# Attention values with the value tile stationary, two heads per bank, divided by reciprocal rows that travel through a DRAM scratch tensor

## The chip, the cores and the metric

The kernel runs on 1 core of one Trainium2 chip. The metric is device time in microseconds (us), the median of several runs. The span of a profiled execution is the stretch from its first to its last recorded instruction. Engines are named as in the profile: PE (TensorE matmul), PEld (TensorE weight load), DVE (VectorE), ACT (ScalarE), POOL (GpSimd), SP (SyncE, which issues the loads).

## The reference, cut to what matters

A trunk of two layers over 256 tokens of width 1024. Each layer is a feed-forward block (width 2816), a token mixer and a second feed-forward block; the mixer of the first layer is latent attention, that of the second a state-space scan. The change lies in the attention, 16 heads, 96 features for queries and keys and 64 for values:

```python
def one_block(args):          # two blocks of 128 queries
    q_blk, i = args
    s = einsum('bhqd,bhkd->bhqk', q_blk, kt) * scale
    s = where(k_pos[None, :] <= q_pos[:, None], s, -inf)
    p = softmax(s, axis=-1)
    return einsum('bhqk,bhkd->bhqd', p, vt)
...
return o.reshape(Bn, S, H * Dv) @ w_o
```

The mixer's result is the 256 x 1024 attention output times a 1024 x 1024 matrix `w_o`.

## The kernel before, in words

Activations are kept as features by tokens (128 features on the partitions, 256 tokens along the row). Large products split both operands into a high and a low half and take three matmuls (`mm3`: high by high, high by low, low by high). Weights come in 1 MiB loads on SP's queue, are cast by ACT (L206) and their low half is formed by DVE (L207). The conditioning vectors of later blocks are worked out beside all this in pieces of one DVE instruction each (`ada_half`, L237).

Order of the work: each engine runs a fixed list of instructions in order. That list is laid out when the kernel is built, by a planner that goes by its own estimate of when each instruction's inputs are ready; the order of the code is the priority, not the order itself. The helper lines L295 and L300 hold every matmul and every transpose, L206 and L207 every split into halves.

The attention runs in turns `turn(t)`, one head begun per turn. Head h gets its scores in turn h (`scores`: queries by keys, into one PSUM bank), its softmax in turn h+1 (`softmax`: row maxima on DVE, exponentials on ACT, whose accumulators give the denominators `DEN`, queries on the partitions), its three transposes of 128 x 128 probabilities in turn h+2 (`probs_t`), the copy of these out of PSUM in turn h+3 (`probs_evac`), and its products with the values in turn h+4 (`values`).

`values(h)` holds the transposed probabilities stationary (128 x 128) and moves 64 columns of the values: three products, whose result is queries by features. Four heads (a "quad") share one bank. `o_evac(quad)` (turn 4 quad + 8) takes the reciprocal of the denominators (L1058) and multiplies the whole bank by it (L1060), `o_t(quad)` turns the result into features by queries with four transposes, and `o_split(quad)` splits it into halves (L206, L207) that enter the product with `w_o`.

Turns 0 to 18 are written ahead of `down`, turns 19 to 22 are hooks inside it. `down(s, 8, ...)` makes the eight 128-row chunks m of `w_o`'s product; each has eight steps k, and step k takes `OT[k]`, two heads' output. Chunks 0 and 1 first do steps k = 0 to 5, with the hooks after every second step, and after all hooks their steps 6 and 7, which need the last quad. Chunks 2 to 7 follow whole. After each chunk `leave_chunk` (L460) and `enter_chunk` (L409 to L411, L399) update the residual and prepare the next block on DVE, ACT and POOL.

PSUM has eight banks, one tag for all uses. The scan of the second layer has a product `ymm`, L1309 to L1317, that the change resembles: it holds 64 columns of a value-like tile stationary and writes one head of a pair to partitions 0 to 63 of a bank and the other to 64 to 127.

Of the kernel before, what the change touches and what calls it, by code (L numbers as in the profile page):

```python
# [7 lines left out]
F32 = mybir.dt.float32  # L8
F32R = mybir.dt.float32r
# [3 lines left out]
ALU = mybir.AluOpType  # L13
# [3 lines left out]
T = 256  # L17
# [5 lines left out]
HEADS = 16  # L23
# [31 lines left out]
class Piece:  # L55


    def __init__(self, hi, lo):
        self.hi, self.lo = hi, lo
# [5 lines left out]
class Trunk:  # L65
    def __init__(self, ctx, tc, a, out):
        self.tc, self.nc, self.a, self.out = tc, tc.nc, a, out
        self.p = ctx.enter_context(tc.tile_pool(name="sb", bufs=1))
        self.ps_pool = ctx.enter_context(
            tc.tile_pool(name="ps", bufs=8, space=bass.MemoryType.PSUM))  # L70
        self.uid = 0
        self.pin = False

# [635 lines left out]

    def mla_setup(self):  # L710
        nc = self.nc
        self.qag = self.cst["latg"]
        rowg = self.cst["qkg_row"].rearrange("p (a d) -> p a d", a=2)
        inv = self.cst["inv"]
# [8 lines left out]
                                in1=inv.rearrange("p (o d) -> p o d", o=1).broadcast_to([128, 2, 16]), op=ALU.mult)  # L723
# [92 lines left out]
    def mla(self, s):  # L816
        nc = self.nc
# [27 lines left out]
        q = [self.latent(qp[0], R, 2)]  # L845
# [5 lines left out]
        for c in range(2):  # L851
            self.transpose(out=krp[:, c * 32:(c + 1) * 32], in_=kr[0:32, c * 128:(c + 1) * 128],
                                identity=self.ident[0:32, 0:32])
# [62 lines left out]
        KT, QT, V = [], {}, [[None, None], [None, None]]  # L916

        def kt_evac(banks):
            for b in banks:
                KT.append(self.heads_evac(b, self.gcol[0:96, 0:1]))  # L920
# [75 lines left out]
        QT[0] = [self.heads_evac(b, None) for b in qb]  # L996
        q_evac(1, 1, p1)

        SC, PB, PTs, O, DEN, OT, ON, OB = {}, {}, {}, {}, {}, [], {}, {}

        def scores(h):
            quad, hh = divmod(h, 4)
# [10 lines left out]
        def softmax(h):  # L1013
            quad, hh = divmod(h, 4)
            if hh == 0:
                DEN[quad] = self.small([128, 2, 4], "den", 3)
            cq = CQ[quad]
            ps = SC[h]
            mx = self.small([128, 2], "mx", 4)
            nc.vector.reduce_max(out=mx[:, 1:2], in_=ps[:, 0:256], axis=AX.X)  # L1020
            nc.vector.reduce_max(out=mx[:, 0:1], in_=ps[:, 256:384], axis=AX.X)
            nc.vector.scalar_tensor_tensor(out=mx, in0=mx, scalar=-1.0, in1=cq[:, :, hh], op0=ALU.mult, op1=ALU.mult)
            P = self.t3()
            for c, sl in ((1, slice(0, 256)), (0, slice(256, 384))):
                nc.scalar.activation(out=P[:, sl], in_=ps[:, sl], func=AF.Exp, bias=mx[:, c:c + 1],  # L1025
                                     scale=cq[:, c, hh:hh + 1], accum_out=DEN[quad][:, c, hh:hh + 1])
            SC[h] = P

        def probs_t(h):
            P = SC.pop(h)  # L1030
            pp = PB[h] = self.bank()
            for b in range(3):
                self.transpose(out=pp[:, b * 128:(b + 1) * 128], in_=P[:, b * 128:(b + 1) * 128],
                                    identity=self.ident)

        def probs_evac(h):
            PTs[h] = self.t3()
# [2 lines left out]
            else:  # L1040
                nc.vector.tensor_copy(out=PTs[h], in_=PB.pop(h)[:, 0:384])  # L1041

        def values(h):
            quad, hh = divmod(h, 4)
            half, h8 = divmod(h, 8)
            if hh == 0:
                O[quad] = self.bank()
            PT = PTs.pop(h)
            hc = slice(h8 * 64, (h8 + 1) * 64)
            o0 = O[quad][:, hh * 64:(hh + 1) * 64]  # L1050
            o1 = O[quad][:, 256 + hh * 64:256 + (hh + 1) * 64]
            self.matmul(o1, PT[:, 0:128], V[0][half][:, hc], start=True, stop=False)
            self.matmul(o1, PT[:, 128:256], V[1][half][:, hc], start=False, stop=True)
            self.matmul(o0, PT[:, 256:384], V[0][half][:, hc], start=True, stop=True)

        def o_evac(quad):
            den = DEN.pop(quad)
            nc.vector.reciprocal(out=den, in_=den)  # L1058
            t = ON[quad] = self.slot()
            nc.vector.tensor_tensor(  # L1060
                out=t.rearrange("p (c h d) -> p c h d", c=2, d=64),
                in0=O.pop(quad).rearrange("p (c h d) -> p c h d", c=2, d=64),
                in1=den.rearrange("p c (h o) -> p c h o", o=1).broadcast_to([128, 2, 4, 64]), op=ALU.mult)

        def o_t(quad):
            t = ON.pop(quad)
            ps = OB[quad] = self.bank()
            for b in range(2):
                for c in range(2):
                    self.transpose(out=ps[:, b * 256 + c * 128:b * 256 + (c + 1) * 128],  # L1070
                                        in_=t[:, c * 256 + b * 128:c * 256 + (b + 1) * 128], identity=self.ident)

        def o_split(quad):
            ps = OB.pop(quad)
            hi, lo = self.slot(F32R), self.slot(F32R)
            self.split_pair(hi, lo, ps)
            for b in range(2):
                OT.append((hi[:, b * T:(b + 1) * T], lo[:, b * T:(b + 1) * T]))

        def turn(t):  # L1080

            quad, hh = divmod(t, 4)
            nq = quad + 2
            if t < HEADS and hh == 0:
                if quad == 0:
                    kt_evac(b3)
                    q_rstd(1)
                if nq < 4:
                    turn.p0 = q_proj(nq, 0)
            if 0 <= t - 3 < HEADS:  # L1090
                probs_evac(t - 3)
            if 0 <= t - 1 < HEADS:
                softmax(t - 1)
            if t >= 8 and t % 4 == 0:
                o_evac(t // 4 - 2)
            if t >= 10 and t % 4 == 2:
                o_split(t // 4 - 2)
            if t < HEADS:
                scores(t)
            if nq < 4:  # L1100
                if hh == 1:
                    q_evac(nq, 0, turn.p0)
                    turn.p1 = q_proj(nq, 1)
                if hh == 2:
                    q_evac(nq, 1, turn.p1)
                if hh == 3:
                    q_rstd(nq)
            if 0 <= t - 2 < HEADS:
                probs_t(t - 2)
            if 0 <= t - 4 < HEADS:  # L1110
                values(t - 4)
            if t >= 9 and t % 4 == 1:
                o_t(t // 4 - 2)
            if quad + 1 < 4:
                if hh == 1:
                    turn.qb = quad_t(QQ[quad + 1])
                if hh == 2:
                    QT[quad + 1] = [self.heads_evac(b, None) for b in turn.qb]

        tail = HEADS + 3  # L1120
        for t in range(tail):
            turn(t)

        def last(t):
            turn(t)
            self.ada_half(2)
        rest = [lambda t=t: last(t) for t in range(tail, HEADS + 7)]
        self.down(s, 8, lambda k: OT[k], rest, 2, 2, 1, MLA_EVERY)


# [513 lines left out]
```

## Time and profile before

| | |
|---|---|
| median of 3 runs | 1076.95 us (1076.59 to 1077.67) |
| profiled execution, its own time | 1077.47 us |
| its span | 1075.7 us |
| PE busy | 1059.3 us, 98% of the span |
| DVE busy | 871.9 us, 81% |
| ACT busy | 617.5 us, 57% |
| POOL busy | 40.0 us, 4% |
| attention turns, by the trace | about 250 to 290 us into the span |

Busy time of PE is modelled: matmuls overlap, so the distance from one group's start to the next group's start is the better measure of what a group costs. In a row of a timeline the number in front is the start, then the length, and "x6" says how many instructions were merged; the bracket tells how long the engine had been idle before it and what ended that. All DMAs of this kernel are issued by SP and run on one queue.

### The profile page before, as it was taken

What the parts mean: (1) busy time and instruction counts of PE and PEld (TensorE: products, weight loads), DVE (VectorE), ACT (ScalarE), POOL (GpSimd) and SP (SyncE); (2) the same over time, 40 slices, a digit from 0 to 9 for tenths busy, and PEclk for the clock granted to TensorE, in tenths of its full rate; (3) what the DMA queues carried; (4) which work ended last, traced back from release to release, by engine and by line L of the source; (5) the groups of instructions that cost most, each with busy time, mean ns of one, the idle gap of its engine ahead of it and who ended that gap; (6) DMA issues with size and microseconds to landing.
All of it is one profiled execution on the core that took longest, in us unless ns stands there. A gap on an engine that the chain in (4) does not pass through costs nothing.

```text
span 1075.7 us, 21725 instructions
## 1 busy us (share of the span) xinstructions
PE 1059.3 (98%) x8814; PEld 1042.9 (97%) x8814; DVE 871.9 (81%) x1551; ACT 617.5 (57%) x1099; POOL 40.0 (4%) x102
## 2 busy tenths in 40 slices
PE   6999999999999999999999999999999999999998
PEld 5999999999999999999999999999999899999998
DVE  5899988889989878766999886599999788756642
ACT  5564544479567454444745444498889566544431
POOL 0000000000010000100000000000210000000000
PEclk9999999999999999999999999999999999999999
DMA  9999898754266887875699887554344454666630
GB/s 349 334 368 347 338 374 310 286 199 150 100 232 225 325 306 292 290 271 199 240 362 350 334 321 257 171 180 157 119 137 157 157 183 171 240 221 217 231 131 21
DMA packets 38264, 259.59 MB, mean 241 GB/s; under 512 B 4370, under 2 KB 5522, under 8 KB 8084
## 3 DMA queue, kind: packets, MB, share of 16 engines
q1 hardware_dynamic: 38164, 258.21, 65.9%
q8 instruction: 69, 1.13, 0.4%
q14 instruction: 31, 0.25, 0.1%
HBM read 257.14 MB, written 1.05 MB: 240 GB/s over the span
## 4 chain that ended last, share of the span: by engine, by line
PE 93%; DMA 3%; DVE 2%; ACT 1%; issue 0%; SPq 0%; ACTq 0%
PE bank L295 92%; DMA raw<-in_adao_dram 3%; PE bank L300 1%; DVE raw L259 1%; DMA raw<-in_xt_dram 0%; ACT sl L813 0%; ACT t L1025 0%; DVE wlo L618 0%; ACT whi L206 0%; DVE ssq L947 0%; ACT t L942 0%; DVE wlo L207 0%; DVE mx L1020 0%; ACT sl L811 0%; DVE t L1041 0%
## 5 line engine op out<-in xcount | busy, mean ns | idle before, releaser
L295 PE MATMUL bank<-sl,whi 128*128 128x256 f32 (+2 forms) x5360 | 954.7, 282 | 5.2 <-ACT sl L652 4.0
L295 PEld LDWEIGHTS bank<-sl,whi 128*128 128x128 f32 (+1 forms) x5360 | 818.0, 188 | 8.6 <-ACT sl L652 5.0
L295 PE MATMUL bank<-sl,wlo 128*128 128x256 f32 (+2 forms) x2680 | 746.3, 280 | 0.0
L206 ACT CAST whi<-raw 128x1024 fp32r<-128x1024 f32 (+1 forms) x329 | 340.8, 1041 | 304.2 <-PE bank L295 217.3
L295 PEld LDWEIGHTS bank<-sl,wlo 128*128 128x128 f32 (+1 forms) x2680 | 503.5, 188 | 0.2
L207 DVE TENSOR_TENSOR wlo<-raw,whi 128x1024 fp32r<-128x1024 f32 (+1 forms) x329 | 398.0, 1214 | 90.4 <-ACT whi L206 88.3
L237 DVE SCALAR_TENSOR_TENSOR raw<-raw,cb 128x1024 f32<-128x1024 f32 x128 | 154.7, 1220 | 25.4 <-DMA raw<-in_adaw_dram 25.2
L329 ACT CAST sl<-t 128x256 fp32r<-128x256 f32 x125 | 48.7, 405 | 32.6 <-DVE t L526 24.4
L330 DVE TENSOR_TENSOR sl<-t,sl 128x256 fp32r<-128x256 f32 x125 | 51.2, 419 | 1.0 <-ACT sl L329 0.7
L460 DVE SCALAR_TENSOR_TENSOR x<-bank,mod,x 128x256 f32<-128x256 f32 x48 | 22.9, 480 | 21.8 <-PE bank L295 21.6
L410 ACT ACTIVATE sl<-x,scol 128x256 fp32r<-128x256 f32 x40 | 20.3, 508 | 33.4 <-DVE x L460 33.3
L526 DVE TENSOR_TENSOR t<-t,bank 128x256 f32<-128x256 f32 x70 | 28.8, 417 | 12.5 <-PE bank L295 12.5
L1164 DVE SCALAR_TENSOR_TENSOR sl<-t,cst,sl 128x256 f32<-128x256 f32 x72 | 35.1, 495 | 0.1
L525 ACT ACTIVATE t<-bank 128x256 f32<-128x256 f32 x70 | 26.0, 380 | 0.0
L295 PE MATMUL bank<-whi,sl 128*128 128x384 f32 (+1 forms) x80 | 24.3, 368 | 0.0
L259 DVE SCALAR_TENSOR_TENSOR raw<-raw,cb 128x1024 f32<-128x1024 f32 x16 | 19.6, 1222 | 5.6 <-DMA raw<-in_adao_dram 5.5
L409 POOL CAST sl<-bspl 128x4 fp32r<-128x4 f32 x40 | 11.8, 343 | 318.7 <-PE bank L295 232.1
L1302 ACT ACTIVATE dec<-sl,nac 128x128 f32<-128x128 f32 x64 | 20.6, 399 | 4.9 <-DVE sl L1291 4.8
L411 DVE SCALAR_TENSOR_TENSOR sl<-x,scol,sl 128x256 fp32r<-128x256 f32 x40 | 19.3, 482 | 4.2 <-ACT sl L410 4.1
L440 POOL TENSOR_TENSOR rr<-rv,mhalf 128x2 f32<-128x2 f32 x11 | 11.2, 1019 | 304.2 <-DVE rv L436 304.2
L423 ACT ACTIVATE t<-t,mod,scol 128x256 f32<-128x256 f32 x32 | 18.4, 596 | 4.0 <-DVE t L422 4.0
L618 DVE TENSOR_TENSOR wlo<-raw,whi 128x1024 fp32r<-128x1024 f32 (+1 forms) x17 | 19.5, 1156 | 0.0
(215 smaller groups left out, 652.8 us busy)
## 6 DMA issues: line engine op xcount, KB each, us to landing
raw<-in_wgu_dram SPq DMA_DIRECT2D x80, 1024.0 KB, 5.6
raw<-in_adaw_dram SPq DMA_DIRECT2D x64, 1024.0 KB, 5.9
raw<-in_wdn_dram SPq DMA_DIRECT2D x44, 1024.0 KB, 6.0
raw<-in_win_dram SPq DMA_DIRECT2D x19, 1024.0 KB, 5.0
raw<-in_wout_dram SPq DMA_DIRECT2D x8, 1024.0 KB, 4.9
raw<-in_wop_dram SPq DMA_DIRECT2D x6, 1024.0 KB, 6.7
raw<-in_adao_dram SPq DMA_DIRECT2D x6, 1024.0 KB, 8.4
raw<-in_mwo_dram SPq DMA_DIRECT2D x4, 1024.0 KB, 4.9
```

Source lines behind the costliest of these rows:

```text
L206: self.nc.scalar.copy(out=hi, in_=raw)
L207: self.nc.vector.tensor_tensor(out=lo, in0=raw, in1=hi.bitcast(F32), op=ALU.subtract)
L237: nc.vector.scalar_tensor_tensor(out=w, in0=w, scalar=1.0, in1=self.cb, op0=ALU.mult, op1=ALU.mult, accum_out=self.mod[:, q, 2 * u + i:2 * ...
L259: self.order(nc.vector.scalar_tensor_tensor(out=w, in0=w, scalar=1.0, in1=self.cb, op0=ALU.mult, op1=ALU.mult, accum_out=self.mod[:, q, c]))
L295: ins = self.nc.tensor.matmul(*a, **k)
L329: self.nc.scalar.copy(out=hi, in_=src)
L330: self.nc.vector.tensor_tensor(out=lo, in0=src, in1=hi.bitcast(F32), op=ALU.subtract)
L460: nc.vector.scalar_tensor_tensor(out=self.x[m], in0=ps[:, 0:T], scalar=self.mod[:, q, m:m + 1], in1=self.x[m], op0=ALU.mult, op1=ALU.add)
L525: nc.scalar.activation(out=tg, in_=pg[:, 0:T], func=AF.Silu)
L526: nc.vector.tensor_tensor(out=tg, in0=tg, in1=pu[:, 0:T], op=ALU.mult)
L1164: nc.vector.scalar_tensor_tensor(out=dst, in0=u[:, t:t + T], scalar=cw[:, t:t + 1], in1=dst, op0=ALU.mult, op1=ALU.add)
L1302: self.order(nc.scalar.activation(out=t[:, j, 2 * c], in_=q[:, o:o + 128], func=AF.Exp, bias=self.nac[:, c, h:h + 1]))
```

## The change

The products are turned round. `values(pair)` takes two heads: the values (128 keys x 64 features) are stationary and the transposed probabilities move, 256 columns for the first 128 keys and 128 columns for the second. The two heads of the pair write partitions 0 to 63 and 64 to 127 of one bank, so the result is features by queries and needs no transpose: `o_t`, `o_split` and their four transposes per quad are gone. `probs_t` writes its three blocks in another order, so that the moving columns are contiguous. A pair is taken in every odd turn from turn 5.

The division must now vary along the row instead of along the partition. `divisors(quad)` (turn 4 quad + 5) takes the reciprocals and sends them from POOL's queue, in two DMAs, to a scratch tensor `dend` in DRAM laid out as head by query: 128 partitions x 4 single values each, 512 pieces of 4 bytes per DMA. Two more DMAs read it back, each row broadcast to 64 partitions (64 partitions x 2 rows of 256 values). `o_evac(quad)` (turn 4 quad + 8, as before) then multiplies two banks by these rows and splits the product. The hooks are turns 17 to 20 instead of 19 to 22.

```diff
-            self.matmul(o1, PT[:, 0:128], V[0][half][:, hc], start=True, stop=False)
-            self.matmul(o1, PT[:, 128:256], V[1][half][:, hc], start=False, stop=True)
-            self.matmul(o0, PT[:, 256:384], V[0][half][:, hc], start=True, stop=True)
...
+        def values(pair):
+
+            ps = O[pair] = self.bank()
+            hs = [2 * pair, 2 * pair + 1]
+            PT = [PTs.pop(h) for h in hs]
+            for c in range(2):
+                for j, h in enumerate(hs):
+                    half, h8 = divmod(h, 8)
+                    self.matmul(ps[j * 64:(j + 1) * 64, c * 128:T], V[c][half][:, h8 * 64:(h8 + 1) * 64],
+                                PT[j][:, c * 256:256 + c * 128], start=(c == 0), stop=(c == 1))
+        def divisors(quad):
+
             den = DEN.pop(quad)
             nc.vector.reciprocal(out=den, in_=den)
...
+            d = self.dend[quad]
+            for c in range(2):
+                nc.gpsimd.dma_start(out=d.rearrange("h c q -> c q h")[c], in_=den[:, c])
+            t = DB[quad] = self.slot()
+            for j in range(2):
+                nc.gpsimd.dma_start(out=t[j * 64:(j + 1) * 64].rearrange("p (i l) -> p i l", i=2),
+                                    in_=d.rearrange("(i j) c q -> j i (c q)", j=2)[j].partition_broadcast(64))
+
+        def o_evac(quad):
+            t = self.slot()
+            for i in range(2):
+                ps = O.pop(2 * quad + i)
+                nc.vector.tensor_tensor(out=t[:, i * T:(i + 1) * T], in0=ps[:, 0:T], in1=DB[quad][:, i * T:(i + 1) * T],
+                                        op=ALU.mult)
+                if quad == 3:
+                    OT.append(self.split_act(t[:, i * T:(i + 1) * T]))
+            if quad < 3:
+                hi, lo = self.slot(F32R), self.slot(F32R)
+                self.split_pair(hi, lo, t)
...
-        tail = HEADS + 3
+        tail = HEADS + 1
...
-        rest = [lambda t=t: last(t) for t in range(tail, HEADS + 7)]
+        rest = [lambda t=t: last(t) for t in range(tail, HEADS + 5)]
```

## Rows read from the trace of the kernel before

**Rows 1.** The page: busy shares, forty slices, the chain that ended last.

```profile
PE 1059.3 (98%) x8814; PEld 1042.9 (97%) x8814; DVE 871.9 (81%) x1551; ACT 617.5 (57%) x1099; POOL 40.0 (4%) x102
PEclk9999999999999999999999999999999999999999
PE 93%; DMA 3%; DVE 2%; ACT 1%; issue 0%; SPq 0%; ACTq 0%
```

**Rows 2.** Busy time by stretch: length, PE, PEld, DVE, ACT, POOL, clock, DMA.

```profile
260.00:265.00 5.00, 4.98 (x39) 4.88 (x40) 4.28 (x15) 4.44 (x16) 0.00 (x0) 1.00 0.01 3
270.00:275.00 5.00, 4.95 (x42) 4.77 (x42) 4.82 (x20) 3.48 (x13) 0.00 (x0) 1.00 0.01 2
285.00:290.00 5.00, 4.72 (x43) 4.72 (x44) 4.62 (x10) 2.63 (x10) 0.67 (x7) 1.00 0.01 3
290.00:295.00 5.00, 5.00 (x45) 5.00 (x44) 4.88 (x10) 0.84 (x2) 0.00 (x0) 1.00 0.82 249
```

**Rows 3.** Chain that ended last, in order of time, attention's first turns.

```profile
257.86 0.47 DVE t L1041
...
267.93 0.42 DVE mx L1020
```

**Rows 4.** PE's timeline: value products of two turns, four transposes of `o_t`.

```profile
275.00 0.78 PE L295 MATMUL bank<-sl,t 128*128 128x64 f32 x6
276.76 0.78 PE L295 MATMUL bank<-sl,t 128*128 128x64 f32 x6
277.38 0.87 PE L295 MATMUL bank<-sl,sl 96*128 96x256 f32 x4
280.81 0.61 PE L300 MATMUL bank<-ident,sl 128*128 128x128 f32 x4
281.26 0.82 PE L295 MATMUL bank<-sl,sl 96*128 96x256 f32 x4
281.91 0.27 PE L295 MATMUL bank<-maskq,identb 128*128 128x256 bf16 x1
```

**Rows 5.** PE's timeline in the scan: one pair of `ymm` and its neighbours.

```profile
759.92 0.28 PE L295 MATMUL bank<-sl,wlo 128*128 128x256 f32 x1
760.12 0.87 PE L295 MATMUL bank<-dec,sl 128*64 128x256 f32 x8
760.93 0.50 PE L295 MATMUL bank<-sl,whi 128*128 128x256 f32 x2
761.26 0.29 PE L295 MATMUL bank<-sl,wlo 128*128 128x256 f32 x1
```

**Rows 6.** Groups by line and shape, 254 to 294 us: count, busy us, mean ns.

```profile
L295 PE MATMUL bank<-sl,t 128*128 128x64 f32 x96 | 13.0, 264 | 0.2 <-DVE t L1041 0.2
L237 DVE SCALAR_TENSOR_TENSOR raw<-raw,cb 128x1024 f32<-128x1024 f32 x6 | 7.2, 1219 | 0.0
L1060 DVE TENSOR_TENSOR sl<-bank,den 128x512 f32<-128x512 f32 x4 | 2.7, 687 | 0.2 <-PE bank L295 0.2
L300 PE MATMUL bank<-ident,sl 128*128 128x128 f32 x16 | 2.5, 273 | 0.0
```

**Rows 7.** The page's groups: 128x256 casts, halves and products from PSUM; POOL's power.

```profile
L329 ACT CAST sl<-t 128x256 fp32r<-128x256 f32 x125 | 48.7, 405 | 32.6 <-DVE t L526 24.4
L330 DVE TENSOR_TENSOR sl<-t,sl 128x256 fp32r<-128x256 f32 x125 | 51.2, 419 | 1.0 <-ACT sl L329 0.7
L526 DVE TENSOR_TENSOR t<-t,bank 128x256 f32<-128x256 f32 x70 | 28.8, 417 | 12.5 <-PE bank L295 12.5
L440 POOL TENSOR_TENSOR rr<-rv,mhalf 128x2 f32<-128x2 f32 x11 | 11.2, 1019 | 304.2 <-DVE rv L436 304.2
```

**Rows 8.** POOL's power, the single line: ns at least, median, most.

```profile
L440 POOL TENSOR_TENSOR rr<-rv,mhalf x11: 690/701/1773, 213.2 to 891.2; 128x2 f32<-128x2 f32 x11
```

**Rows 9.** DMA issues of the whole run: KB each, median us to landing.

```profile
raw<-in_mwo_dram SPq DMA_DIRECT2D x4, 1024.0 KB, 4.9
out_dram<-x SPq DMA_DIRECT2D x8, 128.0 KB, 2.5
raw<-in_win_dram SPq DMA_DIRECT2D x1, 512.0 KB, 3.6
posi<-in_pos_dram SPq DMA_DIRECT2D x1, 1.0 KB, 8.9
```

**Rows 10.** DVE's timeline: reciprocal and multiplication of the first and last quad.

```profile
262.68 0.20 DVE L1058 RECIPROCAL den<-den 128x8 f32<-128x8 f32 x1
270.31 0.68 DVE L1060 TENSOR_TENSOR sl<-bank,den 128x512 f32<-128x512 f32 x1
287.07 0.20 DVE L1058 RECIPROCAL den<-den 128x8 f32<-128x8 f32 x1
289.88 0.69 DVE L1060 TENSOR_TENSOR sl<-bank,den 128x512 f32<-128x512 f32 x1
292.76 0.69 DVE L207 TENSOR_TENSOR sl<-bank,sl 128x512 fp32r<-128x512 f32 x1
293.44 1.22 DVE L207 TENSOR_TENSOR wlo<-raw,whi 128x1024 fp32r<-128x1024 f32 x1
```

**Rows 11.** PE's timeline where `down` goes from step 5 to step 6.

```profile
293.00 0.40 PE L295 MATMUL bank<-sl,whi 128*128 128x256 f32 x2
293.24 0.28 PE L295 MATMUL bank<-sl,wlo 128*128 128x256 f32 x1
293.36 0.40 PE L295 MATMUL bank<-sl,whi 128*128 128x256 f32 x2
293.71 0.64 PE L295 MATMUL bank<-sl,whi 128*128 128x256 f32 x4
```

**Rows 12.** Waits of the whole run: DVE in front of a DMA's landing.

```profile
DVE raw L237 <- DMA raw<-in_adaw_dram: 25.2, 13, 4.1
```

## What the change should do to the time

> **What bounds the kernel now.** I read the page first: PE is busy for 98% of the span at the full clock level, 93% of the chain that ended last lies on it, and DVE comes second with 81% [rows 1]. So the question is what the attention costs PE. The table of stretches answers it for the stage: from 260 us on PE is busy for 4.7 to 5.0 of every 5 us, and DVE, with 4.3 to 4.9, is nearly as full [rows 2]. But part of DVE's load there is filler: six pieces of conditioning (L237, 1.22 us each, 7.2 us in all) are put wherever the planner sees room [rows 6]. In the first turns, up to about 260 us and again at 268 us, the chain runs over DVE and ACT instead [rows 3], so work taken from PE before that brings nothing. A turn lasts 276.76 - 275.00 = 1.76 us [rows 4].
>
> **Values, per pair of heads.** Before, six PE instructions make one head's products (96 in all [rows 6]), and the group that starts at 276.76 is followed by the next at 277.38: 0.62 us per head [rows 4], 1.24 us per pair. The new form has a twin in the trace, the scan's pair product: two heads, 64 stationary columns, moving 256 and then 128 columns, eight instructions. It starts at 760.12, the next group at 760.93: 0.81 us [rows 5]. Around it something is lost. At the pitch of the split matmuls (293.36 - 293.00 = 0.36 us for three [rows 11], 0.12 each) the instruction after the one at 759.92 was due at 760.04, which is 0.08 us at the entry; and the two matmuls after the group take 761.26 - 760.93 = 0.33 us instead of 0.24, which is 0.09 us at the exit. Together 0.98 us per pair. Eight pairs save 8 x (1.24 - 0.98) = 2.1 us.
>
> Do the two heads overlap in the array? The scores say what one instruction costs alone: 281.91 - 281.26 = 0.65 us for two instructions of 256 and two of 128 columns [rows 4]. Two heads one after the other would be 1.30 us, and the twin's eight instructions take 0.81, so they do overlap, though not fully (that would be 0.65). The Trainium skill, TensorEngine Tiling (Array Packing), Key Properties, says that different tiles run weight loads and matmuls in parallel and that a change of the tiling mode drains the engine. The trace agrees with both, by the 0.81 us and the 0.08 and 0.09 us; the 2x of its table, 0.65 us per pair as an estimate, would save 4.7 us in place of 2.1.
>
> **Transposes.** The four of a quad start at 280.81 and what follows at 281.26: 0.45 us; 16 in all [rows 4, 6], so 1.8 us. The reordered `probs_t` costs nothing: same count, same shapes. PE's work falls by 2.1 + 1.8 = 3.9 us. About 0.95 us of that belongs to the first quad (two pairs 0.5, its transposes 0.45), which lies where DVE and ACT lead [rows 3]: worth nothing. 1.2 us lies behind the last softmax (two quads' transposes 0.9, the last heads' values 0.3), where the end is set by the last quad's division, below. 1.7 us remain as a gain ahead of it.
>
> **DVE and ACT.** A quad had one product of 128x512 at 687 ns and now has two of 128x256 at 417 ns: +0.15 us, 0.6 us for four [rows 6, 7]. The reciprocal and the split stay, the split only changes its source. I cost this at nothing, since 7.2 us of filler can move out of the stage [rows 6]; if DVE finds no such room, 0.6 us.
>
> **The way through DRAM.** This is new, and the trace has neither a DMA of POOL nor one of pieces this small. The chain is: reciprocal, two writes issued, both landed, two reads issued, both landed, product. Both landings are in series, since the reads fetch what the writes left. Nearest rows for a landing: a store of 128 KB lands 2.5 us after its issue; loads of 512 and 1024 KB take 3.6 and 4.9 us, so one of no size takes 3.6 - 1.3 = 2.3 us [rows 9]. Lower end 4.8 us. Upper end: a load of 1 KB that landed after 8.9 us behind other traffic [rows 9], twice, 17.8 us. For the issue on POOL the nearest row is its small power: 1.02 us in the mean, 1.77 us at most [rows 7, 8]. I take the dear price for the two writes, which consist of 512 single values each, and the mean for the reads: 2 x 1.77 + 2 x 1.02 = 5.6 us. Chain: 4.8 + 5.6 = 10.4 us. I choose it inside 4.8 to 17.8 because nothing in the trace lets POOL do anything on 512 pieces faster than its own arithmetic on two columns.
>
> The Trainium skill, DMA: Bandwidth & Descriptors, Anatomy of one DMA and Rules for kernel authors, gives about 2.0 us fixed per DMA from GpSimd and says that a strided last dimension becomes one descriptor per element. By its fixed part alone the two serial trips are an estimate of 4.0 us, and the chain would fit its slot; no run here shows that.
>
> What waits: `o_evac` on DVE, and behind it in DVE's order the next heads' row maxima and copies, on which ACT and PE wait. Behind the reads on POOL stand only later pads and casts, needed a block later.
>
> Quads 0 to 2: before, the reciprocal ended at 262.88 and the product began at 270.31 [rows 10], a slot of 7.4 us. The chain is 3.0 us late; a turn of 1.76 us between stages is slack; 1.2 us reach PE, three times 3.7 us. The two lines stand next to each other in the code and 7.4 us apart in the trace, so the planner does move them; it may set the product later. I take half: +1.9 us. Ends: 0, and 3 x 8.6 = 26 us.
>
> Last quad: the reciprocal ends at 287.27 [rows 10]. With 10.4 us for the chain, and product 0.42, cast 0.40, low half 0.42 [rows 7], step 6 can start at 298.9; before, it started at 293.71 [rows 11]. That is 5.2 us later, less the 1.7 us by which everything arrives sooner: +3.5 us. PE has run dry at 293.71 - 1.2 = 292.5 on this scale, but chunk 2's steps 0 to 5 need no last quad: 18 matmuls at 0.12 us, 2.1 us that can be drawn forward. Against that speaks that a late weight half was only begun at 293.44 [rows 10]; chunk 3 would be another 2.1 us. I take one chunk: +1.4 us (ends -2.9 in the whole, all hidden, and +3.5).
>
> **Sum** against the profiled execution of 1077.47 us: +1.9 + 1.4 = +3.3, 1080.8 us. The median of the runs lies 0.5 us lower: 1080.3 us.
>
> **Rivals.** (1) The transfer is hidden: with a chain under about 6 us no quad waits, and the last one is ready at 287.27 + 6 + 1.24 = 294.5, so that chunk 2's 2.1 us fill PE from 292.5. Then 1.7 + 1.2 = 2.9 us are gained: 1074.1 us, faster. For it: the 4.8 us floor, a nearly idle DMA from 285 to 290 us [rows 2]. Against it: four issues in a row on one queue, and thirteen places where DVE already stood before a DMA that landed later than planned, 25.2 us in all [rows 12]. It decides at a chain of about 7.4 us. (2) Break-even: a chain of 8.9 us (every issue 1.02 us) is late by less than a turn for quads 0 to 2, and the last quad comes at 297.4 - 293.71 - 1.7 - 2.1 = -0.1: 1077 us. (3) Transfer of 14 us: quads 3 x 4.8 / 2 = 7.2, end +5.0: 1089 us. (4) The pairs don't overlap here: a pair then takes 1.30 + 0.17 = 1.47 us, 0.23 more than before, and eight of them eat the 1.8 us of the transposes. PE gains nothing, up to 3.9 us less than in my sum: 1084 us; the twin speaks against it [rows 5].
>
> **How the numbers follow.** About 0.2% (2.2 us) is what a measurement of this kernel can tell from no change. Transfer late, my forecast, with (3) and (4) as its long side: 0.49 (forecast 0.37, (3) 0.09, (4) 0.03). Break-even: 0.27. Hidden: 0.24. The range runs from the hidden case, 1073.8, to a chain of about 14 us, 1089; the cases beyond are under 2 in 10. The likeliest case's own range is 1079 to 1085 us.
>
> **What would show it.** Right: a pair takes about 0.8 us on PE between its neighbours; the reads land about 10 us after the reciprocal; DVE's idle time in front of the product is put down to a DMA; PE, which had no gap after 286 us, has one of 1 to 4 us ahead of step 6. Wrong: landing within 7 us, or later matmuls of chunks 2 and 3 standing ahead of step 6 so that PE has no gap, or DVE's wait falling where PE has work.

## The result, and the profile after

The changed kernel takes 1123.55 us (1122.87 to 1125.98), the kernel before beside it 1077.57 us (1076.59 to 1079.33): a ratio of 1.0424, 95% interval 1.0413 to 1.0435. That it would be slower was forecast; the time lies 43 us above the forecast and 35 us above the end of its range.

The page after, in the order of [rows 1]: busy time, PE's granted clock in forty slices, the chain that ended last, and the group of the new product.

```profile
PE 1072.4 (96%) x8766; PEld 1044.9 (93%) x8766; DVE 873.3 (78%) x1556; ACT 618.1 (55%) x1100; POOL 48.0 (4%) x118
...
PEclk9999999999688999999999999999999999999999
...
PE 86%; DMA 9%; DVE 3%; ACT 1%; issue 1%; POOL 0%; SPq 0%; POOLq 0%; DVEq 0%; ACTq 0%
...
L1072 DVE TENSOR_TENSOR sl<-bank,sl 128x256 f32<-128x256 f32 x8 | 3.0, 420 | 44.2 <-DMA sl<-dend 44.2
```

DVE stood for 44.2 us in front of the product, and a DMA ended all of it. The group it answers to before had waited 0.2 us [rows 6]. The chain's DMA share went from 3% to 9%. There is a second thing that [rows 1] did not have: three slices in which PE's clock is below full. And PE is busy 13 us longer although it has 48 instructions fewer.

Where in the run? POOL's small power at about 234 us and the next one after it bracket the attention with its `w_o` product; I call this the stage. POOL's timeline, before:

```profile
233.22 1.33 POOL L440 TENSOR_TENSOR rr<-rv,mhalf 128x2 f32<-128x2 f32 x1 [6.12 <-DVE rv L436]
...
318.74 0.69 POOL L440 TENSOR_TENSOR rr<-rv,mhalf 128x2 f32<-128x2 f32 x1 [19.89 <-DVE rv L436]
```

and after:

```profile
234.29 1.33 POOL L441 TENSOR_TENSOR rr<-rv,mhalf 128x2 f32<-128x2 f32 x1 [6.30 <-DVE rv L437]
...
363.53 1.69 POOL L441 TENSOR_TENSOR rr<-rv,mhalf 128x2 f32<-128x2 f32 x1 [26.91 <-DVE rv L437]
```

The stage takes 85.52 us before and 129.24 after: 43.7 of the 46 us are in it. (Each stage in this document is read from one execution. The rest of the span is 2.3 us longer here, and 0.4 to 3.7 us longer in the variants below. Part of that lies ahead of the stage, which starts 1.1 us later here though the work up to it is the same, and executions of the kernel before differ by 2.7 us; the rest is not explained.)

The steps of one transfer stand in two timelines of after. POOL's: start, length of the issues, what it issued, the idle time before. DVE's: reciprocal and product of the first and the last quad (compare [rows 10]).

```profile
263.57 1.69 POOL L1062 DMA_DIRECT2D dend<-den  x2 [27.94 <-DVE rst L780]
275.92 1.20 POOL L1065 DMA_DIRECT2D sl<-dend  x2 [10.66 <-DMA dend<-den]
```

```profile
263.05 0.20 DVE L1059 RECIPROCAL den<-den 128x8 f32<-128x8 f32 x1
281.39 0.76 DVE L1072 TENSOR_TENSOR sl<-bank,sl 128x256 f32<-128x256 f32 x2 [10.69 <-DMA sl<-dend]
...
322.01 0.19 DVE L1059 RECIPROCAL den<-den 128x8 f32<-128x8 f32 x1
340.03 0.76 DVE L1072 TENSOR_TENSOR sl<-bank,sl 128x256 f32<-128x256 f32 x2 [12.89 <-DMA sl<-dend]
```

From the reciprocal's end at 263.25 to the product at 281.39 are 18.1 us, where the forecast had 10.4. The table of DMA issues (KB each, median us to landing) and POOL's wait say which half is at fault:

```profile
sl<-dend POOLq DMA_DIRECT2D x8, 128.0 KB, 5.0
...
dend<-den POOLq DMA_DIRECT2D x8, 2.0 KB, 10.1
```

```profile
POOL sl L1065 <- DMA dend<-den: 31.6, 3, 11.1
```

The writes of 2 KB take 10.1 us to land, twice as long as the reads that move 128 KB.

PE's timeline shows where PE stood for it, once per quad (7.7, 10.4, 6.9 and 8.4 us, 33.2 in all):

```profile
281.87 1.94 PE L301 MATMUL bank<-ident,t 128*96 128x128 f32 x8 [7.67 <-DVE sl L1072]
...
304.43 0.69 PE L301 MATMUL bank<-ident,t 128*128 128x128 f32 x2 [10.36 <-ACT t L1027]
...
322.80 0.58 PE L296 MATMUL bank<-sl,whi 128*128 128x256 f32 x1 [6.86 <-ACT sl L207]
...
340.95 1.44 PE L296 MATMUL bank<-sl,whi 128*128 128x256 f32 x5 [8.35 <-ACT sl L330]
```

Last, the table of stretches (length, PE, PEld, DVE, ACT, POOL, clock, DMA share, GB/s; compare [rows 2]):

```profile
265.00:270.00 5.00, 4.92 (x33) 3.52 (x32) 4.54 (x19) 5.00 (x15) 0.25 (x1) 1.00 0.94 32
...
275.00:280.00 5.00, 0.00 (x0) 0.00 (x0) 0.00 (x0) 0.00 (x0) 1.20 (x2) 0.65 0.70 197
280.00:285.00 5.00, 3.13 (x13) 2.72 (x13) 3.61 (x15) 1.21 (x4) 0.30 (x1) 0.50 0.04 11
```

While the writes are under way the DMA engines show a busy share of 0.94, though they move only 32 GB/s. That share is not the writes' own. The table by queue for the same 5 us (packets, MB, share) puts most of it on SP's queue, where a `w_o` load of 1024 KB takes 15.3 us to land; POOL's queue is q0:

```profile
q1 hardware_dynamic: 19, 0.16, 86.9%
q0 software_dynamic: 64, 0.00, 7.3%
```

From 275 to 280 us all compute engines stand still, and when PE starts again its granted clock is 0.50, the lower of its two levels (1.2 GHz).

### The profile page after: what moved, and what is told of

Read it like the earlier page. It is cut to its first block, busy times and chain, and to the rows that moved or that the text cites. A ratio compares the mean times of both kernels' runs of the same rounds, so it can differ in the third digit from the quotient of the medians.

```text
span 1121.7 us, 21668 instructions
## 1 busy us (share of the span) xinstructions
PE 1072.4 (96%) x8766; PEld 1044.9 (93%) x8766; DVE 873.3 (78%) x1556; ACT 618.1 (55%) x1100; POOL 48.0 (4%) x118
## 4 chain that ended last, share of the span: by engine, by line
PE 86%; DMA 9%; DVE 3%; ACT 1%; issue 1%; POOL 0%; SPq 0%; POOLq 0%; DVEq 0%; ACTq 0%
PE bank L296 85%; DMA dend<-den 4%; DMA raw<-in_adao_dram 3%; DMA sl<-dend 2%; DVE raw L260 1%; PE bank L301 0%; DMA raw<-in_xt_dram 0%; DVE wlo L619 0%; ACT sl L815 0%; POOL dend L1062 0%; DVE sl L1072 0%; POOL sl L1065 0%; DVE wlo L208 0%; ACT whi L207 0%; DVE mx L1022 0%
## 5 line engine op out<-in xcount | busy, mean ns | idle before, releaser
L208 DVE TENSOR_TENSOR wlo<-raw,whi 128x1024 fp32r<-128x1024 f32 (+1 forms) x329 | 397.4, 1213 | 96.9 <-ACT whi L207 96.0
L238 DVE SCALAR_TENSOR_TENSOR raw<-raw,cb 128x1024 f32<-128x1024 f32 x128 | 154.5, 1218 | 14.3 <-DMA raw<-in_adaw_dram 14.3
L301 PE MATMUL bank<-ident,t 128*96 128x128 f32 (+2 forms) x116 | 21.0, 301 | 18.8 <-ACT t L1027 11.0
L1072 DVE TENSOR_TENSOR sl<-bank,sl 128x256 f32<-128x256 f32 x8 | 3.0, 420 | 44.2 <-DMA sl<-dend 44.2
L301 PEld LDWEIGHTS bank<-ident,t 128*96 128x96 f32 (+2 forms) x116 | 14.5, 144 | 24.2 <-ACT t L1027 13.3
L441 POOL TENSOR_TENSOR rr<-rv,mhalf 128x2 f32<-128x2 f32 x11 | 11.8, 1075 | 312.5 <-DVE rv L437 312.5
```

The source lines that it names most:

```text
L208: self.nc.vector.tensor_tensor(out=lo, in0=raw, in1=hi.bitcast(F32), op=ALU.subtract)
L238: nc.vector.scalar_tensor_tensor(out=w, in0=w, scalar=1.0, in1=self.cb, op0=ALU.mult, op1=ALU.mult, accum_out=self.mod[:, q, 2 * u + i:2 * ...
L301: ins = self.nc.tensor.transpose(*a, **k)
```

## Experiments

Four theories were to be told apart. (A) The transfer is the whole loss, and its price lies in the 512 single values per write. (B) The loss is elsewhere: contention with the loads, or the values form itself. (C) The price is POOL's way of issuing. (D) The lower clock after a stop is a loss of its own.

**1. Without the transfer.** The product multiplies by a resident tile, so the division is left out.

```diff
-            d = self.dend[quad]
...
+            DB[quad] = self.cb
```

> The changed kernel with the four DMAs per quad left out: the reciprocal is still taken, but the product multiplies by a resident tile (the conditioning row), so the division is left out of the result. Theory A (the loss of 46 us is the wait for the way through DRAM, and the halved clock after each wait): the waits of DVE ahead of the product, 44.2 us in the changed kernel, go to zero, PE's idle time falls back to that of the kernel before, and the gain on PE that was worked out (3.9 us, 2.9 of it of use) shows: 1073 to 1076 us. Rival B (the two-head value products themselves, with their change of tiling and two banks per quad, hold PE up): the time stays over 1080 us.

Measured: 1081.11 us, ratio 1.0029 (1.0015 to 1.0042); the stage takes 86.47 us. So 42.8 of the stage's 43.7 us hang on the transfer: (A) against (B). But the 3 us that PE should have gained are not there, and the time lies 5 us above the expected range. PE's timeline of this kernel shows why:

```profile
277.72 0.65 PE L296 MATMUL bank<-t,sl 128*64 128x256 f32 x2
278.30 0.33 PE L301 MATMUL bank<-ident,t 128*128 128x128 f32 x1
278.56 0.86 PE L296 MATMUL bank<-t,sl 128*64 128x256 f32 x6
279.35 0.92 PE L296 MATMUL bank<-sl,sl 96*128 96x256 f32 x4
...
281.73 0.87 PE L296 MATMUL bank<-t,sl 128*64 128x256 f32 x8
282.53 0.92 PE L296 MATMUL bank<-sl,sl 96*128 96x256 f32 x4
```

The second pair is whole: 282.53 - 281.73 = 0.80 us for its eight instructions. The first has a head's transpose inside: 279.35 - 277.72 = 1.63 us, which is 0.72 more than 0.80 and the 0.11 of a transpose. The planner split six of the eight pairs, five with a transpose inside and the last with products of `w_o` (in the changed kernel seven of eight). Theory (E): the splits eat the gain, 6 x 0.7 = 4 us.

**2. Writes that nobody waits for.** As 1, but the writes are issued. The division is left out.

> As e1_no_transfer, but the two writes of single values per quad are issued and nobody waits for them; the reads are left out, and so is the division. Theory A: within 1 us of e1_no_transfer, since only the wait costs. Rival C (the 512 small pieces fill the 16 DMA engines and hold up the weight loads, and that costs the time): 5 us or more above e1_no_transfer, with DVE or ACT waiting for weight loads. The landing of the writes should be 9 to 11 us as in the changed kernel.

Measured: 1081.29 us, the same as 1; the writes land after 10.4 us:

```profile
dend<-den POOLq DMA_DIRECT2D x8, 2.0 KB, 10.4
```

The writes do hold up a weight load: from 265 to 270 us the DMA engines move 20 GB/s, in run 1 210. What they take from other transfers costs nothing, though; only waiting for them does. They are not slow because PE and DVE stand still. Nor is a load beside them the reason: quad 2's writes are issued at 282.1 us, the DMA engines move 2 GB/s from 280 to 290 us without a packet of SP's queue, and these writes take 10.4 us as well.

**3. The same bytes in fewer pieces.** As 2, with one write of 128 pieces of 32 bytes per quad. The division is left out, and the scratch holds the values in another order.

```diff
-            for c in range(2):
-                nc.gpsimd.dma_start(out=d.rearrange("h c q -> c q h")[c], in_=den[:, c])
+            nc.gpsimd.dma_start(out=d.rearrange("h c q -> (h c q)").rearrange("(q l) -> q l", l=8),
+                                in_=den.rearrange("p c h -> p (c h)"))
```

> As e2_writes_unwaited, but the scratch is laid out so that a quad's reciprocals go in one DMA of 128 pieces of 32 bytes instead of two of 512 pieces of 4 bytes; nobody reads them and the division is left out. If the number of pieces sets the landing (1024 pieces in about 12 us for the pair of writes), this one lands after 2 to 4 us. If it is a fixed price of POOL's DMAs or of a write to DRAM, it stays at 8 us or more.

```profile
dend<-den POOLq DMA_DIRECT2D x4, 4.0 KB, 1.8
```

Measured, in one execution: 1.8 us to land, 1080.14 us for the whole. The same 4 KB in an eighth of the pieces land in a sixth of the time: the pieces are the price. Their number and their size change together here, so it is not shown which of the two sets it.

**4. Another queue.** All four DMAs issued by ACT.

```diff
...
-                nc.gpsimd.dma_start(out=d.rearrange("h c q -> c q h")[c], in_=den[:, c])
+                nc.scalar.dma_start(out=d.rearrange("h c q -> c q h")[c], in_=den[:, c])
...
```

> The changed kernel with its four DMAs per quad issued by ACT instead of POOL. If the pieces of 4 bytes set the price, the writes land after 9 us or more here too, and the time is about that of the changed kernel, 1115 to 1140 us, since ACT itself now stands before the reads. If issuing from POOL is what is dear, the writes land within 4 us and the time is under 1100 us.

```profile
dend<-den ACTq DMA_DIRECT2D x8, 2.0 KB, 11.3
```

Measured, in one execution: 1127.49 us, writes 11.3 us. (C) falls: the writes are slow on the other queue and from the other engine too. The Trainium skill, DMA: Bandwidth & Descriptors, Rules for kernel authors, says that DMAs of different issuing engines share the same DMA engines; the landing of 11.3 us against 10.1 is in line with that.

**5. Rows first, then the write.** PE turns the 128 x 8 reciprocals, DVE copies the eight rows out of PSUM, and one write stores them as 8 x 512 bytes. (The denominators change their layout for it, in lines not shown.)

```diff
...
-            for c in range(2):
-                nc.gpsimd.dma_start(out=d.rearrange("h c q -> c q h")[c], in_=den[:, c])
+            ps = self.bank()
+            self.transpose(out=ps[0:8, 0:128], in_=den.rearrange("p h c -> p (h c)"), identity=self.ident)
+            rows = self.small([8, 128], "dens", 2)
+            nc.vector.tensor_copy(out=rows, in_=ps[0:8, 0:128])
+            nc.gpsimd.dma_start(out=d.rearrange("h c q -> (h c) q"), in_=rows)
```

> The changed kernel, its result unchanged, with one step more: the reciprocals of a quad are turned by PE into 8 rows of 128 and written as 8 pieces of 512 bytes in one DMA; the reads stay. Theory A1 (the chain is dear because of the 4-byte pieces of the write): the write lands after about 2.5 us instead of 10, the chain falls from 18 to about 10 us, DVE waits 2 to 4 us per quad instead of 11, and the time is 1080 to 1092 us. Rival D (any DMA of POOL that writes to DRAM and is read back costs this much): the write still lands after 8 us or more, and the time is above 1110 us.

```profile
sl<-dend POOLq DMA_DIRECT2D x8, 128.0 KB, 2.9
dend<-dens POOLq DMA_DIRECT2D x4, 4.0 KB, 1.7
```

```profile
DVE sl L1075 <- DMA sl<-dend: 6.5, 3, 4.7
```

Measured: 1090.19 us, ratio 1.0114 (1.0098 to 1.0131), stage 95.84. The writes land in 1.7 us, the reads in 2.9, DVE's wait falls from 44.2 to 6.5 us, and 33 us come back. (A) holds. These landings are near the 2.5 and 2.3 us that the forecast took, and the chain from reciprocal to product is 7.8 to 11.5 us, near its 10.4. Yet the kernel is 12 us slower than before, not 3: in the stage PE stands for 7.6 us (1.2 before) and is busy for 88.3 (84.3 before), at a granted clock of 0.66 to 1.00. Of the standing 5.6 us lie in front of the new transposes, which the change itself does not have, so this run does not test the forecast's sum at its own chain.

**6. One transfer instead of four.** Quads 0 to 2 multiply by the resident tile (their division is left out), the last quad goes through DRAM as in the change.

```diff
+            if quad < 3:
+                DB[quad] = self.cb
+                return
```

> The changed kernel with the transfer for the last quad alone; the first three quads multiply by a resident tile, so their division is left out. Theory A: one stop in place of four: DVE waits 10 to 13 us once, at the last quad, and the time is that of e1_no_transfer plus a quarter of the loss, 10 to 15 us: 1084 to 1090 us. If the planned order covers the last quad's wait with chunks 2 and 3 of the output product, as the prediction took in part, it is below 1080 us.

Measured: 1095.42 us, ratio 1.0164 (1.0149 to 1.018); stage 101.72, which is 15.2 us above 1. So the last quad's transfer alone costs 15.2 us, a third of the loss where a quarter and at most 1090 us had been expected, and the other three add 129.24 - 101.72 = 27.5 to it (by the medians of the whole 14.3 and 28.1). PE's timeline across the stop:

```profile
298.36 0.28 PE L296 MATMUL bank<-sl,wlo 128*128 128x256 f32 x1
311.72 1.44 PE L296 MATMUL bank<-sl,whi 128*128 128x256 f32 x5 [13.08 <-ACT sl L330]
312.96 0.41 PE L296 MATMUL bank<-sl,wlo 128*128 128x256 f32 x1
...
313.60 0.41 PE L296 MATMUL bank<-sl,wlo 128*128 128x256 f32 x1
...
316.49 0.28 PE L296 MATMUL bank<-sl,wlo 128*128 128x256 f32 x1
...
316.84 0.28 PE L296 MATMUL bank<-sl,wlo 128*128 128x256 f32 x1
```

From one `wlo` instruction to the next (three instructions) it takes 313.60 - 312.96 = 0.64 us behind the stop and 316.84 - 316.49 = 0.35 once the clock is back. The table of stretches has the granted clock:

```profile
305.00:310.00 5.00, 0.00 (x0) 0.00 (x0) 0.00 (x0) 0.00 (x0) 0.00 (x0) 0.50 0.84 285
310.00:315.00 5.00, 3.28 (x15) 3.28 (x16) 2.24 (x8) 1.90 (x4) 1.04 (x8) 0.50 0.02 3
315.00:320.00 5.00, 5.00 (x40) 5.00 (x39) 4.88 (x9) 4.96 (x9) 0.00 (x0) 0.89 0.40 136
```

The slow pitch lasts from 311.72 to about 316: 4.2 us for work that at the pitch of 0.35 would take 4.2 x 0.35 / 0.64 = 2.3, an estimate. 13.1 + 1.9 = 15.0, nearly the whole of the 15.2. (D) holds as a second loss behind each stop.

**7. Dividing earlier, without any transfer.** The probabilities are multiplied by the reciprocals before they are turned, where the queries still lie on the partitions; on POOL in one kernel, on DVE in the other (`nc.vector`). `divisors` and the product in `o_evac` go, and every quad's result is split straight out of PSUM in two pieces.

```diff
...
+            r = self.small([128, 2], "rden", 4)
+            nc.vector.reciprocal(out=r, in_=DEN[quad][:, :, hh])
+            for c, sl in ((1, slice(0, 256)), (0, slice(256, 384))):
+                nc.gpsimd.tensor_scalar(out=P[:, sl], in0=P[:, sl], scalar1=r[:, c:c + 1], scalar2=None, op0=ALU.mult)
...
```

> The two-head value products kept, the division moved to the probabilities, which are multiplied by their reciprocal on POOL ahead of the transposes, where it varies by partition; no DMA, no rows, result unchanged. Theory A: the gain on PE shows if POOL keeps up with a turn of 1.7 us: 1073 to 1077 us. If POOL takes longer than a turn for 128 x 384 elements, PE waits for it and the time is above 1080 us.

> As e9_norm_pool, with the multiplication on DVE: some 0.5 to 0.6 us more of DVE per head, 8 to 9 us in all, less the 3.4 us of the products that are gone. If DVE has room in the stage (7.2 us of filler), 1074 to 1077 us; if DVE becomes the bound there, 1078 to 1084 us.

Measured: 1100.18 us on POOL, ratio 1.0195 (1.0173 to 1.0217), stage 104.69; 1090.70 on DVE, ratio 1.0101 (1.0079 to 1.0124), stage 92.61. The groups and the waits of the one on POOL:

```profile
L1032 POOL TENSOR_SCALAR t<-t,rden 128x256 f32<-128x256 f32 (+1 forms) x32 | 27.5, 871 | 45.6 <-DVE rden L1030 37.5 <-DVE rst L778 4.5 <-DVE mx L1024 3.6
...
PE bank L301 <- POOL t L1032: 12.3, 11, 3.0
```

and the group of the one on DVE:

```profile
L1032 DVE TENSOR_SCALAR t<-t,rden 128x256 f32<-128x256 f32 (+1 forms) x32 | 8.9, 316 | 0.0
```

POOL takes 871 ns where DVE takes 316, but on DVE the 8.9 us meet an engine that was nearly full [rows 2], PE stands 9.8 us in front of the transposes for them, and the time lies above the 1078 to 1084 us expected for that case. Either is dearer than the division of before; what the other form of the split adds is not told apart.

**8. Pairs held together.** As 1 (division left out), but the planner has to leave the four products of a pair in their order; this is theory (E) by itself.

```diff
+                self.pin = True
                 values(t // 2 - 2)
+                self.pin = False
```

> The same work as the kernel without the transfer (the division multiplies by a resident tile, so it is left out in effect), but the four value products of a pair are now held together in their written order; in that kernel a transpose stood inside six of the eight pairs. Theory S: the split costs what the pairs should have saved (a split pair takes 1.63 us with the transpose's 0.10 inside, a whole one 0.80, so about 0.7 us for each of six pairs, 4 us). Then the attention stage gets 3 to 5 us shorter than its 86.5 us there, below the 85.5 us of the kernel before, and the whole lands 3 to 5 us below 1081.1: 1076 to 1078. Rival: the pairs are no dearer split than whole on the path that sets the end, and the gain is lost elsewhere (waits on DVE, the later stages): the stage stays within 1 us of 86.5 and the whole at 1080 to 1082.

PE's timeline of one pair, and POOL's two powers around the stage:

```profile
279.47 0.87 PE L296 MATMUL bank<-t,sl 128*64 128x256 f32 x8
280.27 0.92 PE L296 MATMUL bank<-sl,sl 96*128 96x256 f32 x4
```

```profile
233.39 1.33 POOL L441 TENSOR_TENSOR rr<-rv,mhalf 128x2 f32<-128x2 f32 x1 [6.30 <-DVE rv L437]
...
316.10 0.69 POOL L441 TENSOR_TENSOR rr<-rv,mhalf 128x2 f32<-128x2 f32 x1 [17.92 <-DVE rv L437]
```

Measured: 1076.61 us, ratio 0.9984 (0.9975 to 0.9993). All eight pairs are whole, the stage takes 82.71 us, 3.76 less than in 1 and 2.81 less than before, and the whole 4.5 us less than in 1. (E) holds.

**9. Rows first, with pairs held together, and with a later product.** As 5 with the lines of 8; the second kernel also writes the products of quads 0 to 2 one turn later.

```diff
-            if t >= 8 and t % 4 == 0:
+            if t in (9, 13, 17, 20):
                 o_evac(t // 4 - 2)
```

> The kernel that turns the reciprocals into eight rows before one write of 512-byte rows (1090.2 us), with the value products of a pair held together as well. Theory S: 3 to 5 us less than there, 1085 to 1087. Rival: 1089 to 1091, since PE waits for the transfer in these stretches and the time saved goes into a longer wait.

> As the run with rows and pairs held together, but the product of quads 0 to 2 is written one turn (1.8 us) later, behind the next head's softmax. If what is left of the stop in quads 0 to 2 is only the chain's length against its slot (DVE waited 6.5 us in three places, 4.7 of them at the last quad), the first two of these waits go and 2 to 4 us are saved: 1082 to 1084. If the planner's places and PE's wait for the transpose of the reciprocals rule instead, it stays within 1 us of the run with pairs held together. The last quad's wait of about 5 us stays in either case.

Measured: 1091.54 us, ratio 1.013 (1.0114 to 1.0146), stage 96.54; and 1091.76, ratio 1.0124 (1.011 to 1.0137), stage 98.14. Neither gains anything on 5; the rivals hold both times (the first lies 0.5 us beyond its rival's end). PE's timeline of the first shows a wait that whole pairs cannot remove:

```profile
262.17 0.38 PE L301 MATMUL bank<-ident,den 128*8 128x128 f32 x1 [1.47 <-DVE rst L780]
...
275.73 0.37 PE L301 MATMUL bank<-ident,den 128*8 128x128 f32 x1 [1.46 <-DVE mx L1024]
...
288.21 0.27 PE L301 MATMUL bank<-ident,den 128*8 128x128 f32 x1 [3.45 <-DVE den L1059]
```

PE itself now waits for the reciprocals, in front of their transpose: 6.4 us in these three places. Run 5 had this wait already, with 5.6 us, and only three of its eight pairs were split, so that there was less to gain than in 8. In the stage PE is busy for 1.7 us less than in 5 (86.6 against 88.3) and stands for 2.3 us more (9.9 against 7.6). Moving the product takes DVE's waits for the reads from 7.6 to 3.4 us and doesn't shorten the stage.

**10. Rows made by PE alone.** Nothing is left out and nothing goes through DRAM: each column of reciprocals, broadcast to 64 columns, is stationary, the identity moves; ACT copies the bank, DVE multiplies by it. Pairs held together.

```diff
...
+                    for j in range(2):
+                        self.matmul(ps[j * 64:(j + 1) * 64, i * 256 + c * 128:i * 256 + (c + 1) * 128],
+                                    den[:, c, 2 * i + j:2 * i + j + 1].broadcast_to([128, 64]),
+                                    self.ident, start=True, stop=True)
+            t = DB[quad] = self.slot()
+            nc.scalar.copy(out=t, in_=ps)
...
```

> No transfer and nothing left out: PE makes the rows itself. Each reciprocal column, broadcast to 64 columns, is the stationary operand and the identity the moving one, eight such products of 128 columns per quad, held together with a pair's value products; ACT copies the bank of 512 columns, and the product on DVE reads it. The pairs are held together as in the run without a transfer, whose stage took 82.7 us against 85.5 before. Theory: the whole loss hung on the transfer, so without one the change is worth what PE saves less what the rows cost. Eight products per quad, at 0.11 us for one of 128 columns (four transposes take 0.45) and with the overlap of two heads seen in the value pairs (0.81 of 1.30), are 0.5 to 0.6 us per quad, 2.2 us in all, of the 2.8 us gained there: a stage of 84.5 to 85.5 us and 1077 to 1079, the same as before within what can be told. Rival: a chain from reciprocal over PE and ACT to the product (some 2 us, ACT's copy of 512 columns in it) stops the last quad as the transfer did, or the added 0.6 us per quad on ACT delays the exponentials: stage above 87 us, 1080 or more.

```profile
268.60 1.09 PE L296 MATMUL bank<-ident,den 128*64 128x128 f32 x16
269.52 0.82 PE L296 MATMUL bank<-t,sl 128*64 128x256 f32 x8
```

Measured: 1082.37 us, ratio 1.0042 (1.0028 to 1.0055), stage 86.10. The theory's mechanism holds and its size does not. From 262 to 300 us PE has no idle time above 0.44 us, so the stop that the rival named does not come, and the stage stays below its 87 us; the whole lies where it had put it, above 1080. The rows of a quad take 269.52 - 268.60 = 0.92 us, not 0.5 to 0.6: 3.7 us in all, and 82.71 + 3.7 = 86.4 explains the stage. 0.92 us are 0.115 for each of the eight products, the price of 0.11 without the gain that I took for the overlap of two heads. Four transposes are four instructions [rows 4], though, and eight of these products sixteen, so whether the overlap is missing or each product is dearer is not told apart. This is the best full version of the change I found. The kernel before is still 4 us faster; 0.6 us of that lie in the stage, and the other 3, spread over the rest of the span, are not explained.

## Why the prediction was wrong

The stage's 43.7 us, each term the difference of two runs above:

| term | forecast | measured | from |
|---|---|---|---|
| values and transposes, pairs whole | -2.9 | -2.8 | 8 against before |
| pairs split by the planner | 0 | +3.8 | 1 against 8 |
| transfer, quads 0 to 2 | +1.9 | +27.5 | after against 6 |
| transfer, last quad | +4.3 | +15.2 | 6 against 1 |

(The forecast's last line is its +1.4 for the last quad, freed of the 2.9 us of gain that it holds. The transfers were put back in one order only, the last quad first; in the changed kernel itself PE stands 24.9 us for quads 0 to 2 and 8.4 for the last.)

**Values and transposes: right.** A whole pair takes 0.80 us, the scan's 0.81 [rows 5]. The last reciprocal of run 8 starts 285.61 - 233.39 = 52.22 us behind the stage's first power, before 287.07 - 233.22 = 53.85 [rows 10]: 1.6 us sooner, where the forecast had 1.7. The total of -2.8 also fits the sentence that the first quad's share is worth nothing; by the medians of the whole the gain is 1.6 us (1076.61 against 1078.16).

**The split: missed in the main case.** I priced a pair from the scan, whose group is whole, though I had written that the list is laid out by a planner. In the scan the groups are pinned to their order; in the attention they are not. Before the change a transpose inside a value group cost nothing extra: the one at 280.30 us stands in a group that takes 280.81 - 280.13 = 0.68 us, against 0.62 + 0.11 apart. Now it falls between two half-width products, and such a pair takes 1.63 - 0.11 = 1.52 us. That is about the price of rival (4), 1.47 us, and the +3.8 us its 3.9, for another reason than it gave: whole pairs do overlap (0.80 us), but only one of the changed kernel's eight is whole. Whether a split pair is dear by the change of width or by the overlap that it loses is not told apart.

**The landing of the writes: the step that failed.** I took 2.5 us from a store of 128 KB [rows 9], a row of the same direction but of large pieces, while the issue, the term that I did link to the 512 values, got the dear price. It is the other way round: two write issues took 1.69 us and two read issues 1.20, 2.9 instead of 5.6, and landing took 10.1 and 5.0 instead of 4.8 for both. Runs 2 to 5 put this on the pieces. Two writes of 512 values need 10.1 us, 128 pieces 1.8, eight rows 1.7. By these, an estimate: 896 further pieces in 8.3 us, some 9 ns for each. The Trainium skill, DMA: Bandwidth & Descriptors, Rules for kernel authors, says that a strided last dimension becomes one descriptor per element. No view here counts descriptors; the landing of 10.1 us for 512 values against 1.8 for 128 pieces is in line with it. The 2.0 us per DMA of the same page, Anatomy of one DMA, fit the few pieces (1.7 and 1.8 us) and not the many (10.1). I cited both and let only the fixed part enter the estimate.

**Choice inside the bounds: wrong, and the range cut short.** The ends of 4.8 and 17.8 us are those of the two landings alone, while the chain of 10.4 that I set between them holds 5.6 us of issues: its landings stood at their lower end. Both landings together took 15.1. The end of 26 us for quads 0 to 2 was there as well, beside the 27.5 measured. But the range stopped at a chain of 14 us, because I held what lies beyond for less than 2 in 10, without a row that spoke against it.

**Halved because the planner may move the product: wrong.** In the changed kernel 18.1 us of chain less 10.69 of wait leave a slot of 7.4, the number of [rows 10], and the next two quads have 7.3 and 8.2: the product was not moved out of the way of the chain. That 7.4 fits all three is in part luck. In the kernel before it was the first quad's slot alone; quads 1 and 2 had 4.2 and 1.2 us (DVE's timeline). Unhalved and with the measured chain the forecast's own formula holds for the standing: waits of 10.69, 10.99 and 9.64 us, less a turn of 1.76 each, are 26.0 us, and PE stood for 24.9 at these places. The 27.5 of the table is another sum: 8.2 us of it are longer busy time (95.2 us in the stage against 87.0 in run 6), which the formula does not have.

**Last quad: mechanism right, size off.** PE does draw chunks forward (in run 6 it works until 298.6) and then stands, as described, but for 13.1 us, where the text named a gap of 1 to 4. That stop is run 6's, where the chain takes 22.1 us: the writes land after 11.8 us and the reads after 7.6, these beside loads at 129 to 285 GB/s. In the changed kernel the last chain takes 17.8 us and PE stands for 8.4.

**The clock: not in the forecast at all.** PE is busy 1072.4 us after and 1062.1 in run 1, with the same 8766 instructions: 10.3 us of it, by this modelled busy time, are the price of work done at the lower level behind the stops, but for one more split pair. Of the transfer's 42.8 us some 32 are standing and 10 slow work after it. The Trainium skill, TensorE: Matmul & The Clock Gate, HAM oscillation, describes this: a PE that stood waiting for a DMA starts its next work at the lower clock. The trace agrees, by 0.50 from 280 to 285 us; a forecast that knew its stops would have had to add it.

**Rivals and signs.** Of the rivals, the long transfer (3) has the right mechanism; hidden (1) and break-even (2) needed chains of 6 and 8.9 us, and (4) had the price of the split pairs, as said above. Of the signs that were named, DVE's idle time put down to a DMA appeared as it stands; the reads landed about 18 us after the reciprocal instead of 10; PE's gap ahead of step 6 was 8.4 us instead of 1 to 4; and a pair of about 0.8 us stood in one place of eight.

## What to carry to other kernels

Price a DMA by the pieces it breaks into, not by its bytes or by a row for a large transfer: 4 KB as single values took longer to land than 1 MiB loads did [rows 9]. Where a planner orders the work by its own estimates, a new wait is not moved out of the way just because it is longer on the chip, and instructions that only pay when they stand together must be held together. A stop of PE was dearer here than its length (15.2 us for 13.1 of standing), because the work behind it ran at the lower clock for a while. And a busy share of the DMA engines is worth splitting by queue before it is read: here most of it belonged to a load that the writes held up.

## What of the hardware was not expected

- Writes of 512 single values: 10.1 to 11.8 us to land, on POOL's and on ACT's queue alike; 128 pieces of 32 bytes 1.8 us; eight rows of 512 bytes 1.7 us.
- Beside the writes a 1024 KB load on SP's queue took 15.3 us to land (4.9 in run 1). In run 2, where a load is held up as well, that cost nothing.
- A pair of half-width products with one full-width transpose between them takes 0.72 us more than the pair and the transpose apart (1.63 against 0.80 + 0.11).
- Behind a stop PE was granted 0.50 in the records, and three split matmuls took 0.64 us instead of 0.35 until the clock came back.
